# A scan kernel of two linear-attention mixers: the products of a chunk's last two levels are issued one visit later

## The chip, the cores and the metric

The kernel runs on one core of a Trainium2 chip. The core has a matrix engine (TensorE, PE in the profile; its weight loads are PEld), VectorE (DVE), ScalarE (ACT), GpSimd (POOL), and SyncE (SP), which issues the DMA transfers here. Each engine works through its own list of instructions in order and waits for the others by semaphores. The metric is the time on the device in microseconds (us), the median of several runs.

## What is computed

One layer of a backbone over 2048 latent tokens and 256 context tokens (D_MODEL 1024). After a modulated norm and one large projection, two mixers run in parallel, each in both directions over the tokens: gated linear attention (GLA, with a decay per key channel) and a gated delta rule (GDN). Their outputs are normalised, gated, merged and projected. Cut to the part that the change touches, the GLA recurrence of one direction and head is

```
S_t = diag(exp(g_t)) S_(t-1) + k_t v_t^T          # S: 64 x 128, g_t: log decay of each of the 64 key channels
o_t = q_t S_t
```

The kernel computes it by chunks of 128 tokens: o = (state before the chunk) + A v, where A[t,s] = sum over channels of q_t k_s exp(G_t - G_s), G being the running sum of g. The second direction is the same with the order of the tokens reversed.

## The kernel before

A Python program writes the work of each engine with generators that are woven together, and a scheduler then fixes the order of each engine's list. An order-only dependency can be added by `behind()`.

The time line has a projection (to about 1386 us of the span), the scan stage (`phase_mix`, 1386 to 1760) and the output stage (to the end). The scan stage has one *visit* for each of 16 steps, and in step s the forward scan takes a chunk from the front and the backward scan one from the back, so that in the first half (eight visits) outputs of chunks are written out to memory (`do<-oi`, `do<-og`, L1394) and in the second half, after the *turn*, they are read back (`oi<-do` L1388, `og<-do` L1382), added up and finished (`finish`: sums of squares fsq L1408 on ACT, logarithm and exponential of them L1409 and L1410, scaling on POOL L1411, transposes on PE L1415).

The matrix A of a chunk isn't formed by one product, since exp(G_t - G_s) can't be split into two safe factors over a whole chunk. It is made by *levels* m = 64, 32, 16, 8, 4, 2, 1: at level m, pairs of tokens that lie in neighbouring blocks of m are covered, with the decay taken relative to the border of the two blocks. For each pair of levels `gla_group` sums the gates on PE (L1124, with gates split into a high part gh, L132 on ACT, and a low part gl, L135 on POOL), takes exponentials on ACT (E, L1215), and multiplies them with q on DVE (ql, L1221) and with k on POOL (L1222). `gla_lev` multiplies the two on PE (L1263, four heads of 64 channels by halves of 64 tokens: 8 products a level) and puts each level's part into `own` by a masked copy on DVE (L1274); for m = 64 into `at` on ACT (L1271). Level 1 is done apart: `gla_ones` (transposes of g on PE L1233, exponential on ACT L1235, qk on DVE L1237 and POOL L1238) and `gla_near`, which sums qk with a matrix of ones columns on PE (L1245), puts it into `own` (L1247) and copies `own` to `at` (L1251). The gates' load is `g<-dg` (L1109).

In visit order `gla_step` does: the split of the gates, the chunk's ends (`gla_ends`, L1124, exponential L1133 on ACT), then for the chunk of the visit before `gla_near` and the gated state (`gla_state`, L1326 on PE), then the groups of levels 0-1 and 2-3, the output of the chunk before (`gla_out`, L1345 and L1353), the products of these four levels, then the group of levels 4-5 (m = 4 and 2), `gla_ones`, and the products of levels 4-5. Into this are woven the products of the other mixer (L1055, L1058 on DVE, L1066, L1077, L1087, L1096, L1084 on POOL).

Of the kernel before, what the change touches and what calls it, by code (L numbers as in the profile page):

```python
# [97 lines left out]
class Build:  # L98
# [1142 lines left out]
    def gla_near(self, r):  # L1241
        nc, at, own, w = self.nc, r["at"], r["own"], r["near"]
        pd = self.pe()
        for ct in range(2):
            nc.tensor.matmul(pd[:, 2 * ct:2 * ct + 2], w[:, ct], self.bones, start=True, stop=True)  # L1245
        B = [P, 4, 64]
        nc.vector.copy_predicated(own, self.am[:, len(LEVELS) - 2].unsqueeze(1).broadcast_to(B),  # L1247
                                  pd[:, 0:4].unsqueeze(2).broadcast_to(B))
        for x in range(2):
            half = slice(64 * x, 64 * x + 64)  # L1250
            nc.scalar.copy(at[half, :, half], own[half])  # L1251
# [25 lines left out]
    def gla_step(self, f, b, prev):  # L1277
        nc = self.nc
        self.gla_split(f)
        self.gla_split(b)  # L1280
        f["at"] = f["kp"].tile([P, 4, P], F32, name="at", bufs=1)
        own = f["own"] = f["kp"].tile([P, 4, 64], F32, name="own", bufs=1)
        nc.gpsimd.tensor_tensor(own, self.diag[:, f["c"] - NCTX, :].unsqueeze(2).broadcast_to([P, 4, 64]),
                                self.id64.unsqueeze(1).broadcast_to([P, 4, 64]), op=ALU.mult)
        yield
        self.gla_ends(f)
        yield
        if prev is not None:
            self.gla_near(prev[0])
            S = self.gla_state(prev)  # L1290
            yield
        levs = yield from self.gla_group(f, 0)
        self.gla_ends(b)
        yield
        more = yield from self.gla_group(f, 2)
        self.gla_kt(f)
        self.gla_qe(b)
        yield
        if prev is not None:
            out, done = self.gla_out(prev, S)  # L1300
        self.gla_lev(levs + more, out if prev is not None else None)
        if prev is not None:
            done()
            yield
            yield from self.gla_put(prev)
        yield
        last = yield from self.gla_group(f, 4)
        yield
        self.gla_kt(b)
        f["near"] = self.gla_ones(f)  # L1310
        self.gla_qe(f)
        yield
        self.gla_lev(last)
        yield
        if f["c"] == NCH - 1:
            self.gla_near(f)
        yield
# [580 lines left out]
```

## Time and profile before

| | |
|---|---|
| median of 3 runs | 2127.24 us (2123.59 to 2130.51) |
| the profiled execution | 2126.9 us, its span 2125.1 us, granted clock 0.987 |
| busy over the span | PE 2037.5 us (96%), PEld 1670.0 (79%), DVE 1282.5 (60%), ACT 914.1 (43%), POOL 818.2 (38%) |
| DMA | 346.97 MB, mean 163 GB/s; in the scan stage near 300 GB/s |

In the profile's rows the first number is the start in the span or, in rows of groups, the busy time; then the duration, the engine, the line, the operation with the tile written and the tiles read, the shape and the count; in brackets the engine's idle time just before and what ended it. In the chain of waits (the chain of work that ended last) a row is start, duration, and the engine or transfer with its line. A `DMA` row there is a transfer from its issue to its landing. In tables by window the columns stand in the head row; PEclk is the granted clock of PE as a share, DMA the busy share of the 16 DMA engines.

### The profile page before, as it was taken

What the parts mean: (1) busy time and instruction counts of PE and PEld (TensorE: products, weight loads), DVE (VectorE), ACT (ScalarE), POOL (GpSimd) and SP (SyncE); (2) the same over time, 40 slices, a digit from 0 to 9 for tenths busy, and PEclk for the clock granted to TensorE, in tenths of its full rate; (3) what the DMA queues carried; (4) which work ended last, traced back from release to release, by engine and by line L of the source; (5) the groups of instructions that cost most, each with busy time, mean ns of one, the idle gap of its engine ahead of it and who ended that gap; (6) DMA issues with size and microseconds to landing.
All of it is one profiled execution on the core that took longest, in us unless ns stands there. A gap on an engine that the chain in (4) does not pass through costs nothing.

```text
span 2125.1 us, 40362 instructions
## 1 busy us (share of the span) xinstructions
PE 2037.5 (96%) x15208; PEld 1670.0 (79%) x15208; DVE 1282.5 (60%) x2229; ACT 914.1 (43%) x2208; POOL 818.2 (38%) x746
## 2 busy tenths in 40 slices
PE   5999999999999999999999999899998898999998
PEld 2688888888888888777777777688887786787786
DVE  3814555566667663555555655467677786566776
ACT  3645254555553223444344444355555565002332
POOL 2410122222221104666566665266566655102211
PEclk9999999999999999999999999999999999999999
DMA  8323122222222224444444443688988887898543
GB/s 285 110 87 118 48 61 64 76 62 65 63 72 75 62 73 139 130 135 131 139 155 149 134 136 115 200 294 300 324 293 282 299 282 235 289 311 299 183 146 110
DMA packets 272863, 346.97 MB, mean 163 GB/s; under 512 B 25000, under 2 KB 176796, under 8 KB 272668
## 3 DMA queue, kind: packets, MB, share of 16 engines
q1 hardware_dynamic: 272668, 344.39, 49.2%
q8 instruction: 120, 1.97, 0.4%
q14 instruction: 75, 0.61, 0.1%
HBM read 218.73 MB, written 125.57 MB: 162 GB/s over the span
## 4 chain that ended last, share of the span: by engine, by line
PE 71%; DMA 9%; issue 6%; POOL 5%; DVE 4%; ACT 4%; SPq 1%; DVEq 0%; POOLq 0%; ACTq 0%
PE pz L371 46%; PE pm L1604 3%; DMA g<-dg 2%; PE pz L1604 2%; PE pe L943 1%; PE pl L1002 1%; PE pl L995 1%; PE pl L1003 1%; POOL E L1222 1%; DMA dm<-ga 1%; PE pe L1124 1%; PE pp L1822 1%; PE pq L620 1%; PE pz L1087 1%; PE pz L1077 1%
## 5 line engine op out<-in xcount | busy, mean ns | idle before, releaser
L371 PE MATMUL pz<-hi,wh 128*128 128x512 f32 (+1 forms) x1560 | 621.7, 399 | 1.1 <-DVE hi L134 1.1
L371 PE MATMUL pz<-lo,wh 128*128 128x512 f32 (+1 forms) x1560 | 600.6, 385 | 2.0 <-POOL lo L135 2.0
L371 PE MATMUL pz<-hi,wl 128*128 128x512 f32 (+1 forms) x1520 | 588.9, 387 | 0.0
L371 PEld LDWEIGHTS pz<-lo,wh 128*128 128x128 f32 x1560 | 294.8, 189 | 51.5 <-POOL lo L135 3.9
L371 PEld LDWEIGHTS pz<-hi,wh 128*128 128x128 f32 x1560 | 294.5, 189 | 47.3 <-DVE hi L134 1.7
L371 PEld LDWEIGHTS pz<-hi,wl 128*128 128x128 f32 x1520 | 286.1, 188 | 53.8 <-issue 0.4
L135 POOL TENSOR_TENSOR wl<-w,wh 128x1024 fp32r<-128x1024 f32 x44 | 109.6, 2493 | 436.5 <-ACT wh L132 312.0
L575 DVE SCALAR_TENSOR_TENSOR acc<-zpad,cw,acc 128x1024 f32<-128x1024 f32 x192 | 271.4, 1414 | 6.6
L880 DVE CAST_PREDICATED U<-kit,pl 128x256 f16<-128x256 int32 x216 | 91.2, 431 | 140.5 <-PE pl L1003 136.8
L996 ACT CAST ppb<-pl 128x256 f16<-128x256 f32 x216 | 73.6, 373 | 170.9 <-PE pl L995 158.6
L1604 PE MATMUL pm<-y,wb 128*128 128x512 f32 x480 | 117.7, 396 | 1.3 <-DVE ga L1607 1.2
L135 DVE TENSOR_TENSOR sql<-sq,sqh 128x512 fp32r<-128x512 f32 (+1 forms) x36 | 28.0, 805 | 141.3 <-ACT sqh L132 141.1
L1222 POOL TENSOR_TENSOR E<-E,ak 128x256 f32<-128x256 f32 x96 | 81.3, 866 | 78.1 <-ACT E L1215 40.6
L1604 PEld LDWEIGHTS pm<-y,wb 128*128 128x128 f32 x480 | 89.9, 189 | 23.0 <-DVE ga L1607 1.5
L630 POOL TENSOR_TENSOR acc<-acc,sq 128x512 f32<-128x512 f32 x32 | 51.3, 1611 | 137.8 <-ACT sq L629 89.9
L560 ACT COPY zpad<-pz 128x512 f32<-128x512 f32 x48 | 28.2, 587 | 137.5 <-PE pz L371 137.5
L1215 ACT ACTIVATE E<-pe 128x128 f32<-128x128 f32 x320 | 64.9, 308 | 42.6 <-PE pe L1124 42.1
L1124 PE MATMUL pe<-wt,gh 128*128 128x256 f32 x264 | 74.7, 313 | 4.5 <-ACT E L1133 2.7
L1002 PEld LDWEIGHTS <-Tm 128*128 128x128 f16 x864 | 55.5, 98 | 26.8 <-issue 22.2
L880 DVE CAST_PREDICATED Tm<-kit,pl 128x256 f16<-128x256 int32 x180 | 76.4, 424 | 0.0
L132 ACT CAST wh<-w 128x1024 fp32r<-128x1024 f32 x44 | 46.2, 1050 | 68.3 <-PE pz L371 56.0
L1221 DVE TENSOR_TENSOR ql<-E,q 128x256 f32<-128x256 f32 x96 | 66.9, 723 | 9.1 <-ACT E L1212 7.8
(326 smaller groups left out, 4259.3 us busy)
## 6 DMA issues: line engine op xcount, KB each, us to landing
gd<-dgd SPq DMA_DIRECT2D x32, 768.0 KB, 7.4
w<-in_w_in SPq DMA_DIRECT2D x44, 512.0 KB, 3.8
dgate<-ob SPq DMA_DIRECT2D x128, 128.0 KB, 1.8
qk<-dqkv SPq DMA_DIRECT2D x32, 512.0 KB, 6.1
ga<-dgate SPq DMA_DIRECT2D x64, 256.0 KB, 4.6
x<-in_x SPq DMA_DIRECT2D x28, 512.0 KB, 5.0
dqkv<-acc SPq DMA_DIRECT2D x192, 64.0 KB, 1.6
dgd<-tm SPq DMA_DIRECT2D x36, 256.0 KB, 2.5
```

What stands on the lines that cost most here:

```text
L135: getattr(nc, lo).tensor_tensor(dst_lo, src, dst_hi.bitcast(F32), op=ALU.subtract)
L371: nc.tensor.matmul(ps[:, 0:n], a[:, kk, :], b[:, kk, :], start=(k == 0), stop=(k == last - 1))
L575: nc.vector.scalar_tensor_tensor(acc, src, wcol, acc, op0=ALU.mult, op1=ALU.add)
L630: nc.gpsimd.tensor_tensor(v, v, r, op=ALU.mult)
L880: self.nc.vector.copy_predicated(out, mv, data)
L996: nc.scalar.copy(ppl, pc.rearrange("p h (j i) -> p h j i", i=m))
L1002: nc.tensor.matmul(pu[:, h], Tm[:, h], ppl[:, h], start=True, stop=True)
L1124: self.nc.tensor.matmul(out, g[:, i, ct * P:(ct + 1) * P], self.wt[:, d, cols[0]:cols[1]], start=(j == 0), stop=(j == 1))
L1215: nc.scalar.activation(E[:, ct, li, x].rearrange("p (j e i) -> p e j i", e=2, i=m), s[:, x * P:(x + 1) * P].rearrange("p (e j i) -> p e j ...
L1221: nc.vector.tensor_tensor(ql[:, li], E[:, :, li, 0], q, op=ALU.mult)
L1222: nc.gpsimd.tensor_tensor(E[:, :, li, 1], E[:, :, li, 1], k, op=ALU.mult)
L1604: nc.tensor.matmul(ps, self.wab[j // 2][wi][:, 4 * i + k, (j % 2) * P:(j % 2) * P + P], yy[:, k, :], start=(n == 0), stop=(n == 11))
```

## The change

The products of levels 4-5 (and the two masked DVE copies that follow them) are no longer issued at the end of the chunk's own visit, but in the next visit, inside `gla_near`, behind the two products with the ones columns and ahead of the gated state. The chunk's record keeps the group's result until then (`f["last"]`). For the last chunk, `gla_near` runs at the end of its own visit as before, and takes the products with it. The `behind` of the gated state on the last level product (`self.last_lev`) now means the moved products. In the changed file the lines between L1246 and L1313 have numbers higher by one (L1263 is L1264, L1274 is L1275, L1251 is L1252).

```diff
@@ gla_near
         for ct in range(2):
-            nc.tensor.matmul(pd[:, 2 * ct:2 * ct + 2], w[:, ct], self.bones, start=True, stop=True)
+            mm = nc.tensor.matmul(pd[:, 2 * ct:2 * ct + 2], w[:, ct], self.bones, start=True, stop=True)
+        self.gla_lev(r["last"], mm)
         B = [P, 4, 64]
@@ gla_step
         yield
-        last = yield from self.gla_group(f, 4)
+        f["last"] = yield from self.gla_group(f, 4)
         yield
         self.gla_kt(b)
         f["near"] = self.gla_ones(f)
         self.gla_qe(f)
         yield
-        self.gla_lev(last)
         yield
         if f["c"] == NCH - 1:
             self.gla_near(f)
```

How it moves instructions, in three places. First PE, from the end of one visit to the beginning of the next (lv is the products' PSUM tile, bones the ones columns). Before:

```order
L1055 MATMUL pz<-Sb_17905,qk 128x128
L1233 MATMUL pe<-kf,g_17738 128x128 x4
L1055 MATMUL pz<-Sb_17905,qk 128x128 x3
L1263 MATMUL lv<-ql,E 64x64 x16
L1055 MATMUL pz<-Sb_17919,qk 128x128 x4
L1124 MATMUL pe<-wt,gh_18113 128x256
L1124 MATMUL pe<-wt,gl_18114 128x256
L1124 MATMUL pe<-wt,gh_18113 128x256
L1124 MATMUL pe<-wt,gl_18114 128x256
L1245 MATMUL pe<-bones,qk_18048 128x2 x2
L1326 MATMUL pz<-av,akt 64x128 x8
```

and in the changed kernel:

```order
L1055 MATMUL pz<-Sb_17905,qk 128x128
L1233 MATMUL pe<-kf,g_17720 128x128 x4
L1055 MATMUL pz<-Sb_17905,qk 128x128 x3
L1055 MATMUL pz<-Sb_17919,qk 128x128 x4
L1124 MATMUL pe<-wt,gh_18095 128x256
L1124 MATMUL pe<-wt,gl_18096 128x256
L1124 MATMUL pe<-wt,gh_18095 128x256
L1124 MATMUL pe<-wt,gl_18096 128x256
L1245 MATMUL pe<-bones,qk_18048 128x2 x2
L1264 MATMUL lv<-ql,E 64x64 x16
L1326 MATMUL pz<-av,akt 64x128 x8
```

The block of 16 went past four L1055, the four L1124 of the next chunk's ends, and L1245. In most visits it is this one move; in the first two other products (L652) lie there in the place of L1055.

Second, the turn between the two halves of the scan, on ACT and on SP. ACT before, from one cast of gates to the copies at:

```order
L132 CAST gh_18913<-g_18887 128x256
L1135 COPY dec<-E_18215 128x2
L1215 ACTIVATE E<-pe 128x2x4x16 x2
L1215 ACTIVATE E<-pe 128x2x8x8 x2
L1215 ACTIVATE E<-pe 128x2x4x16 x2
L1215 ACTIVATE E<-pe 128x2x8x8 x2
L132 CAST gh_18497<-g_18469 128x512
L1144 COPY akt<-pe 128x256
L1271 COPY at<-lv 64x2x2x64 x2
```

and in the changed kernel (its tiles bear other numbers):

```order
L132 CAST gh_18895<-g_18869 128x256
L1135 COPY dec<-E_18215 128x2
L132 CAST gh_18479<-g_18451 128x512
L1215 ACTIVATE E<-pe 128x2x4x16 x2
L1215 ACTIVATE E<-pe 128x2x8x8 x2
L1215 ACTIVATE E<-pe 128x2x4x16 x2
L1215 ACTIVATE E<-pe 128x2x8x8 x2
L1144 COPY akt<-pe 128x256
L1272 COPY at<-lv 64x2x2x64 x2
```

The cast of the 128x512 gates went ahead of the eight exponentials. On POOL its counterpart gl (L135) went in the same way ahead of the two E products (L1222) that read these exponentials. SP before, at the same turn (do are the outputs in memory, with the chunk's number, first of oi, the other mixer's output, then of og):

```order
L1394 DMA do_7_14836<-og 128x512
L1394 DMA do_8_14837<-og 128x512
L1388 DMA oi<-do_8_14853 128x512
L1388 DMA oi<-do_7_14852 128x512
L1382 DMA og<-do_7_14836 128x512
L1382 DMA og<-do_8_14837 128x512
L1038 DMA gd<-dgd_8_151 128x1536
L1382 DMA og<-do_9_14838 128x512
L1382 DMA og<-do_6_14835 128x512
L1388 DMA oi<-do_9_14854 128x512
L1388 DMA oi<-do_6_14851 128x512
L1109 DMA g_18469<-dg_191 128x512
```

and in the changed kernel:

```order
L1388 DMA oi<-do_8_14853 128x512
L1394 DMA do_7_14836<-og 128x512
L1394 DMA do_8_14837<-og 128x512
L1388 DMA oi<-do_7_14852 128x512
L1038 DMA gd<-dgd_8_151 128x1536
L1382 DMA og<-do_8_14837 128x512
L1382 DMA og<-do_7_14836 128x512
L1382 DMA og<-do_9_14838 128x512
L1382 DMA og<-do_6_14835 128x512
L1388 DMA oi<-do_9_14854 128x512
L1388 DMA oi<-do_6_14851 128x512
L1109 DMA g_18451<-dg_191 128x512
```

The first reload, `oi<-do_8`, which has to wait for the landing of that chunk's write, went ahead of the two og writes.

Third, a visit of the second half on ACT, from the exponential of `gla_ones` to the first copies to at. Before:

```order
L1408 ACTIVATE fsq,fss<-oi 128x128 x2
L1133 ACTIVATE E_19352<-pe 128x512
L1408 ACTIVATE fsq,fss<-oi 128x128
L1135 COPY dec<-E_19352 128x2
L1409 ACTIVATE fss<-fss,cb 128x4
L1408 ACTIVATE fsq,fss<-og 128x128
L1410 ACTIVATE fss<-fss 128x4
L132 CAST gh_19733<-g_19705 128x512
L1408 ACTIVATE fsq,fss<-og 128x128
L1251 COPY at<-own 64x4x64
```

and in the changed kernel:

```order
L1135 COPY dec<-E_19334 128x2
L1408 ACTIVATE fsq,fss<-oi 128x128 x2
L132 CAST gh_19715<-g_19687 128x512
L1408 ACTIVATE fsq,fss<-oi 128x128
L1409 ACTIVATE fss<-fss,cb 128x4
L1408 ACTIVATE fsq,fss<-og 128x128
L1410 ACTIVATE fss<-fss 128x4
L1252 COPY at<-own 64x4x64
```

The cast went ahead of the last fsq of oi and the first of og; L1133 and L1135, the exponential of the next ends, went up as well. In the visits beside it the same cast moves by none to two fsq.

## The prediction

> **What bounds the kernel now.** I began with the busy time by engine in the window of the scan stage, then read PE's own timeline in one plain visit, then the waits by line, and last the chain of waits with the timelines of ACT, POOL and SP at the places where PE stands still. The stage runs from 1386 to about 1760 us of the span:
>
> ```profile
> core 0: us, PE busy (x) PEld busy (x) DVE busy (x) ACT busy (x) POOL busy (x), PEclk, DMA share, GB/s
> 1386.00:1760.00 374.00, 342.40 (x4548) 316.30 (x4546) 275.58 (x623) 213.89 (x908) 235.19 (x276) 0.98 0.85 294
> ```
>
> PE is busy 342.40 of 374.00 us, so all its standing still together is 31.6 us, and the DMA engines carry 0.85 of what they can. Here is PE, then POOL, in a plain visit of the first half:
>
> ```profile
> 1527.94 0.66 PE L1233 MATMUL pe<-kf,g 128*128 128x128 f32 x4
> 1528.43 0.83 PE L1055 MATMUL pz<-Sb,qk 128*128 128x128 f32 x6
> 1529.20 0.46 PE L1263 MATMUL lv<-ql,E 64*64 64x64 f32 x16
> 1530.01 0.46 PE L1263 MATMUL lv<-ql,E 64*64 64x64 f32 x16 [0.36 <-POOL E L1222]
> 1530.41 1.16 PE L1055 MATMUL pz<-Sb,qk 128*128 128x128 f32 x8
> 1531.32 0.36 PE L1124 MATMUL pe<-wt,gh 128*128 128x256 f32 x1
> ...
> 1531.88 0.51 PE L1245 MATMUL pe<-bones,qk 128*128 128x2 f32 x4
> 1532.31 1.09 PE L1326 MATMUL pz<-av,akt 128*64 128x128 f32 x16
> ...
> 1528.29 1.67 POOL L1222 TENSOR_TENSOR E<-E,ak 128x256 f32<-128x256 f32 x2 [2.56 <-ACT E L1215]
> 1530.39 0.73 POOL L1238 TENSOR_TENSOR qk<-qk,ak 128x256 f32<-128x256 f32 x1 [0.43 <-DVE qk L1237]
> ```
>
> The two L1263 rows are the block that moves (16 products in the code, 32 instructions here). From its start at 1529.20 to the next product at 1530.41 it holds PE for 1.21 us, of which 0.36 is a wait for POOL's second E, so 0.85 is work. The reader should also see that qk, which the ones products of L1245 need, leaves POOL at 1530.39 + 0.73 = 1531.12, while PE comes to L1245 only at 1531.88: 0.76 us of cover. The waits of these two lines over the whole stage:
>
> ```profile
> L1263 PE MATMUL lv<-ql,E 64*64 64x64 f32 x1536 | 35.3, 224 | 8.7 <-POOL E L1222 8.7
> L1245 PE MATMUL pe<-bones,qk 128*128 128x2 f32 x64 | 8.3, 233 | 1.0 <-POOL qk L1238 1.0
> ...
> 1625.13 0.46 PE L1263 MATMUL lv<-ql,E 64*64 64x64 f32 x16 [0.36 <-POOL E L1222]
> ```
>
> 8.7 us is all the waiting of L1263, first four levels included; the moved block has 0.36 in visits of either half of the stage, so about 15 visits x 0.36 = 5.4 us is what the change can take away there.
>
> **The change, part by part.** It adds and removes no instruction; 16 products and two DVE copies a visit go later, and the order of ACT, POOL and SP shifts round them.
>
> *The plain visits.* Without the block PE reaches L1245 at 1531.88 - 1.21 = 1530.67, but qk is ready at 1531.12, so there is a new wait of 0.45 in the place of the old one of 0.36. Then L1245 takes 0.43 (1531.88 to 1532.31) and the block its 0.85: L1326 starts at 1531.12 + 0.43 + 0.85 = 1532.40, where it was 1532.31. That is +0.09 a visit, eight visits +0.7. Against it L1124 comes 1.21 earlier, and the exponentials of the next chunk's ends with it. The bounds are -5.4 (every wait goes and none comes) and +0.7; I take 0, nearer to the row than to the hope. The two DVE copies now follow all eight rhs operations of L1058; the copies that wait for them feed L1345, late in the next visit, and I give them nothing.
>
> *The turn between the two halves, ACT and POOL.* The next rows are ACT, POOL and PE round the cast of one chunk's gates (gh), which waits for a load:
>
> ```profile
> 1583.30 1.47 ACT L1215 ACTIVATE E<-pe 128x128 f32<-128x128 f32 x8 [0.86 <-PE pe L1124]
> 1590.05 0.62 ACT L132 CAST gh<-g 128x512 fp32r<-128x512 f32 x1 [5.29 <-DMA g<-dg]
> ...
> 1584.96 1.77 POOL L1222 TENSOR_TENSOR E<-E,ak 128x256 f32<-128x256 f32 x2
> 1590.74 1.29 POOL L135 TENSOR_TENSOR gl<-g,gh 128x512 fp32r<-128x512 f32 x1 [4.00 <-ACT gh L132]
> ...
> 1590.19 1.11 PE L1263 MATMUL lv<-ql,E 64*64 64x64 f32 x64
> 1591.23 0.38 PE L1124 MATMUL pe<-wt,gh 128*128 128x256 f32 x1
> ...
> 1592.99 0.66 PE L1233 MATMUL pe<-kf,g 128*128 128x128 f32 x4
> ```
>
> Before, eight exponentials and the two E products on POOL are done by 1586.7, and ACT then waits 5.29 us with nothing behind it that anyone needs. Afterwards gh stands ahead of those eight exponentials and gl ahead of those two E. So with the same landing: gl ends at 1592.0, the two E take 1.77 to 1593.8, and the last 32 of PE's 64 products, about half of 1.11, end at 1594.3 where they ended at 1591.23. That is +3.1 for L1233. The lower bound is 0 (if PE is held by something else there; its next load was issued 0.8 us after L1233 ended, which may be slack); I take +2.5.
>
> *The same place, SP.* These are SP's issues, the chain's row for the write of og, the page's row for a write of the same size, and the window of the turn:
>
> ```profile
> 1571.44 1.27 SPq L1394 DMA_DIRECT2D do<-og  x2
> 1576.58 2.02 SPq L1388 DMA_DIRECT2D oi<-do  x2
> 1578.64 0.90 SPq L1382 DMA_DIRECT2D og<-do  x2
> 1583.36 0.38 SPq L1109 DMA_DIRECT2D g<-dg  x1
> 1594.38 2.86 SPq L1109 DMA_DIRECT2D g<-dg  x2
> ...
> 1572.18 6.96 DMA do<-og
> ...
> dgd<-tm SPq DMA_DIRECT2D x36, 256.0 KB, 2.5
> ...
> 1576.50:1580.00 3.50, 3.50 (x39) 3.33 (x38) 2.37 (x9) 1.44 (x4) 1.34 (x2) 1.00 0.68 179
> ```
>
> The first reload of oi was issued at 1576.58, when the write of that chunk had landed. Now it stands ahead of the two og writes, so these are issued about 1577.6 to 1578.2 and not 1571.44 to 1572.18, 6 us later, and the og reloads behind them, and the g of 1583.36 behind those, wait for their landing. With 6.96 for the landing g is 5.6 us later (a gd that now goes first gives 0.4 back); with the 2.5 of the quiet row it is 1.2. I take +2.5, nearer the quiet end, since the DMA share there is 0.68. A sentence on a page: the Trainium skill (Perfetto Trace Analysis, DMA Instruction — HWDGE (DVE, Sync)) says that the completion of a transfer that writes to HBM can be surprisingly late, because the semaphore's update comes behind the confirmed write. By that the landing would stay near the 6.96 of the chain's row, this term would be +5.6 and the sum 2137.5; the 2.5 of the page's row, also a write to HBM, speaks for less.
>
> What follows is bound by that g: the later load that is issued after L1233, its cast, and PE:
>
> ```profile
> 1601.88 0.62 ACT L132 CAST gh<-g 128x512 fp32r<-128x512 f32 x1 [5.03 <-DMA g<-dg]
> 1605.56 1.12 PE L1415 MATMUL pe<-kf,oi 128*128 128x128 f32 x4 [4.39 <-POOL oi L1411]
> 1605.50:1607.30 1.80, 1.74 (x8) 0.50 0.71 274
> ```
>
> ACT waits 5.03 and PE 4.39, so a late L1233 is not made up there; it goes through in full. The last row shows one thing more: after 4.39 us of standing PE's granted clock is 0.50. The new stall of 3 to 8 us at L1263 would bring the same, and PE's products from L1124 to the end of L1233, 1591.23 to 1593.65, are 2.4 us: at half the clock +2.4 at most, 0 if the clock stays; I take +1.0, between the two. The Trainium skill (TensorE: Matmul & The Clock Gate, What's actually happening) says that the clock falls to half after an idle window of about 3.4 us, which runs freely, and comes back after a busy one. The trace agrees in the 4.39; by the rule the whole 2.4 would come with any stall that is safely longer than a window, and the sum would be 2135.8.
>
> *The second half.* There the load of g, ACT's sums of squares (fsq) and POOL's scaling (L1411) set the pace, PE waits for them, and what PE gains in a visit is lost in that wait. ACT, and then the chain:
>
> ```profile
> 1655.40 0.30 ACT L1408 ACTIVATE fsq<-oi 128x128 bf16<-128x128 f32 x1
> ...
> 1656.03 0.29 ACT L1408 ACTIVATE fsq<-og 128x128 bf16<-128x128 f32 x1
> ...
> 1658.13 0.62 ACT L132 CAST gh<-g 128x512 fp32r<-128x512 f32 x1 [1.62 <-DMA g<-dg]
> ...
> 1663.07 1.05 POOL og L1411
> 1664.17 0.66 PE pe L1415 x4
> ...
> 1689.63 1.05 POOL og L1411
> ```
>
> Here the cast waits 1.62 for its load, with the fsq already done. Afterwards it stands one fsq of oi, one of og and two short functions earlier, and these, about 1.0 us (1655.40 to 1656.32, and the last short function), come behind the landing and ahead of the og that releases PE. In the next visit two fsq change sides (0.30 and a read-out each, an estimate of 0.8), in the one after one (0.4), and in the visit before two whose og I take to be covered for the most part (0.3). The sum is +2.5 at most, and 0 if the og products have cover in all of them; the og rows in the chain say that two of them don't, and I take +1.5.
>
> The sum: 0 + 2.5 + 2.5 + 1.0 + 1.5 = +7.5 us on the profiled execution of 2126.9 (span 2125.1, 1.8 around it), 2134.4. The median of the three runs is 2127.24, 0.3 above that execution, so I say 2134. A measurement of this kernel can tell about 0.3%, 6.4 us, from no change: faster is below 2120.9, slower above 2133.6.
>
> **The rivals.** *The new waits are covered and it comes out even.* For it: the block's wait only changes its name (0.36 for 0.45), and the g of the turn may land no later, when the og writes meet an emptier machine. Then the sum is 0 plus at most the second half's 2.5, 2127 to 2129. Against it: the 5.29 in front of the cast, behind which eight exponentials now stand.
>
> *It is faster: the next chunk's ends come 1.21 us sooner.* L1124 and the exponentials behind it move up by the whole block in each visit. If they, and not POOL's qk, set the pace in the first half, seven visits give 7 x 1.21 = 8.5 us, 2118; with only the old waits gone it is 2126.9 - 5.4 = 2121.5. It decides if qk is ready by 1530.7, in the place of 1531.12. Against it stands POOL's row, where qk itself waits 0.43 for DVE; and the loss at the turn would have to stay away.
>
> *It is much slower.* The two delays at the turn add up with their upper values, 3.1 + 5.6 + 2.4, and with the 2.5 and 0.7 they make +14.3, 2141. It decides if the og writes take their 6.96 again.
>
> **How the numbers follow.** The likeliest, delays at the turn and in the second half that go through, gets 0.50 with its own range of 2130 to 2139, of which 0.40 lies above 2133.6. Even: 0.28. Faster: 0.16, of it 0.14 below 2120.9. Much slower: 0.06. So faster 0.14, same 0.10 + 0.28 + 0.02 = 0.40, slower 0.46. The range that leaves out half of the fast end and the last of the slow one is 2121 to 2141.
>
> **What would show it.** In the profile afterwards: L1245 waits about 0.45 for POOL qk in the visits of the first half and the moved block not at all; the eight exponentials of the turn start after the gh that waits for its load, and PE stands 3 us or more within its 64 products there; SP issues the og writes after the first reload of oi, near 1577; the gh of 1601.88 starts about 5 us later; PE's waits for og at L1415 are longer by 0.5 to 1 in the visits after 1650. I am wrong if the g of the turn lands as before, or if L1245 waits for nothing and the visits of the first half are 0.4 us or more shorter each.

## The result, and the profile after

The changed kernel takes 2139.52 us (median of 8 runs, 2134.53 to 2144.58), the kernel before 2129.54 (8 runs, 2120.32 to 2131.70): the ratio is 1.0054, interval 1.0036 to 1.0072. It is slower by 10 us, where the prediction had 2134.0, within its range of 2121 to 2141 but too low. The profiled execution of the changed kernel is the slowest of its runs (span 2142.8, 2144.58 with what lies around it), so its visits hold some 15 us of loss and not 10.

The waits of PE in the scan stage, by line and cause (total us, times, longest), first of the kernel before and then of the changed one:

```profile
PE pe L1415 <- POOL oi L1411: 10.6, 3, 4.4
PE lv L1263 <- POOL E L1222: 8.7, 24, 0.8
PE pe L1415 <- POOL og L1411: 7.7, 6, 2.4
```

```profile
PE pe L1415 <- POOL oi L1411: 10.5, 4, 3.9
PE pe L1415 <- POOL og L1411: 10.2, 10, 3.4
PE pe L1245 <- POOL qk L1238: 7.5, 14, 1.0
PE lv L1264 <- POOL E L1222: 5.6, 12, 1.3
PE pz L1096 <- DVE Sb L1091: 4.1, 1, 4.1
PE pe L1233 <- ACT E L1215: 2.1, 1, 2.1
```

The reader sees two things. The moved products traded one wait for another: L1264's fell by 3.1 us, and L1245's came up from 1.0 to 7.5. (In the timeline no moved product waits any more; what is left at L1264 belongs to the first four levels.) And two large waits are new, one at L1096 and one at L1233, while the waits for og became more.

Where in the stage the time went is read from the start of L1345 (the first products of a visit's output) in PE's timeline. The table gives its start, less that of the kernel before, less the same difference in the first visit. Each row is one execution, and one execution says little: r4_all and s_sp have the same lists on ACT, DVE, POOL and SP up to the turn, and differ by 4.7 us at the eighth visit. So a step of a few us weighs only where several rows agree. The other kernels are explained with the experiments.

| kernel | visit 3 | 4 | 8 | 9 | 10 | 13 | 16 |
|---|---|---|---|---|---|---|---|
| changed | -0.8 | +3.4 | +6.2 | +12.2 | +9.0 | +12.3 | +14.8 |
| changed, cast of the fourth visit put back (r1_v4) | +0.8 | +3.0 | +4.8 | +9.5 | +6.6 | +6.2 | +7.9 |
| changed, cast of the turn put back (r2_turn) | -0.8 | +1.2 | +3.2 | +4.4 | +1.2 | +2.9 | +6.6 |
| changed, four casts of the second half put back (r3_half2) | -0.7 | +2.9 | +4.4 | +9.4 | +6.1 | +2.6 | +2.6 |
| changed, all six casts put back (r4_all) | +0.2 | +0.8 | +3.6 | +7.2 | +3.2 | +0.6 | +2.4 |
| the same, and SP's old order at the turn (s_sp) | +3.0 | +5.2 | +8.3 | +8.3 | +4.5 | +1.2 | +2.8 |
| before, all six casts moved up (x_pull) | -0.7 | +0.5 | +3.5 | +6.1 | +2.0 | +7.2 | +7.8 |
| before, first two casts moved up (x_pull1) | -0.4 | +1.1 | +3.6 | +7.6 | +3.9 | +4.4 | +4.8 |
| before, last four casts moved up (x_pull2) | -0.4 | -0.4 | +2.1 | +2.8 | +3.5 | +8.7 | +7.9 |

The changed kernel is 0.8 us ahead at the third visit, which one execution can't tell from nothing, and then loses in three places. (From the fourth visit to the eighth every row loses 1.5 to 3.1 us, those with nothing changed there too, so that part belongs to the one execution of the kernel before.)

**The fourth visit.** ACT and PE of the changed kernel, with two windows, and then ACT of the kernel before at the same place:

```profile
1464.12 0.62 ACT L132 CAST gh<-g 128x512 fp32r<-128x512 f32 x1 [1.60 <-DMA g<-dg]
1464.65 0.74 ACT L1272 COPY at<-lv 64x256 f32<-64x256 f32 x2
...
1466.26 0.65 PE L1233 MATMUL pe<-kf,g 128*128 128x128 f32 x4 [2.12 <-ACT E L1215]
...
1470.03 1.01 PE L1245 MATMUL pe<-bones,qk 128*128 128x2 f32 x4 [0.33 <-POOL qk L1238]
...
1472.04 1.97 PE L1326 MATMUL pz<-av,akt 128*64 128x128 f32 x16
...
core 0: us, PE busy (x) PEld busy (x) DVE busy (x) ACT busy (x) POOL busy (x), PEclk, DMA share, GB/s
1466.00:1470.00 4.00, 3.44 (x20) 3.15 (x20) 3.95 (x10) 1.96 (x11) 3.25 (x6) 0.69 0.97 309
1470.00:1476.00 6.00, 5.97 (x69) 5.51 (x70) 3.47 (x12) 1.30 (x5) 1.35 (x2) 0.64 1.01 385
```

```profile
1463.71 0.75 ACT L1271 COPY at<-lv 64x256 f32<-64x256 f32 x2
...
1466.36 0.71 ACT L132 CAST gh<-g 128x512 fp32r<-128x512 f32 x1
```

The cast of the gates has got ahead of the far copies in ACT's list (the two copies to at for level m = 64, L1272). Its load hasn't landed, so ACT stands 1.60 us, and the copies, the exponentials behind them and PE's L1233 stand with it (2.12 us). Then the granted clock falls: 0.69 from 1466 to 1470, so it fell ahead of the wait of 0.33 at L1245, and 0.64 in the next stretch, where L1326 takes 1.97 us and not 1.09. The visit is 4.2 us longer than before.

**The turn.** ACT, DVE, PE, a window of PE, and the cast of the next visit:

```profile
1595.04 0.62 ACT L132 CAST gh<-g 128x512 fp32r<-128x512 f32 x1 [6.82 <-DMA g<-dg]
1595.56 1.45 ACT L1215 ACTIVATE E<-pe 128x128 f32<-128x128 f32 x8
...
1596.53 0.74 DVE L1221 TENSOR_TENSOR ql<-E,q 128x256 f32<-128x256 f32 x1 [5.14 <-ACT E L1215]
1597.20 0.68 DVE L1091 TENSOR_TENSOR Sb<-Sb,pz 128x512 f32<-128x512 f32 x1
...
1597.93 2.08 PE L1096 MATMUL pz<-vn,gd 128*128 128x128 f32 x8 [4.14 <-DVE Sb L1091]
...
1597.90:1603.60 5.70, 5.67 (x49) 5.45 (x53) 2.19 (x4) 0.37 (x1) 2.90 (x3) 0.50 0.50 175
...
1611.86 0.62 ACT L132 CAST gh<-g 128x512 fp32r<-128x512 f32 x1 [0.91 <-DMA g<-dg]
```

The eight exponentials stand behind the cast, as forecast. But PE isn't stopped at its level products: DVE is, since its ql waits 5.14 us for those exponentials, and the other mixer's Sb (L1091) is queued behind ql on DVE; PE stops at L1096, which needs Sb, for 4.14 us. Then it runs at half clock for 5.7 us. The visit loses 6.0 us, and the next gives back 3.2, since its cast waits only 0.91 us for its load, where it waited 5.03. The net of the two visits is +2.8 here, +1.8 and +1.7 in the two other executions with this order on ACT (r1_v4, r3_half2), and -2.0, -0.4 and -3.8 in the three with the cast put back (r2_turn, r4_all, s_sp). In r4_all the visit itself still loses 3.6, so not all of the 6.0 is the cast's.

SP's issues there:

```profile
1581.41 0.32 SPq L1388 DMA_DIRECT2D oi<-do  x1
1581.82 0.86 SPq L1394 DMA_DIRECT2D do<-og  x2
...
1586.61 1.75 SPq L1382 DMA_DIRECT2D og<-do  x4
...
1589.56 0.38 SPq L1109 DMA_DIRECT2D g<-dg  x1
...
1606.63 0.98 SPq L1109 DMA_DIRECT2D g<-dg  x2
```

The og writes come 10 us later than in the kernel before (5.7 of which the stage was late already), but the og reloads follow 4.8 us behind their issue, where it took 7.2. The g of 1583.36 is issued 6.2 us later, 0.5 more than the stage's own delay. But it lands sooner: the cast that waits for it starts at 1595.04 and not 1590.05, 5.0 us later, 0.7 less than the stage's delay.

**The second half.** A visit near 1700 of the changed kernel, the cast and PE, and then the one of the kernel before:

```profile
1694.86 0.62 ACT L132 CAST gh<-g 128x512 fp32r<-128x512 f32 x1 [3.60 <-DMA g<-dg]
...
1698.11 0.66 PE L1415 MATMUL pe<-kf,oi 128*128 128x128 f32 x4 [3.49 <-POOL oi L1411]
...
1700.71 0.66 PE L1415 MATMUL pe<-kf,og 128*128 128x128 f32 x4 [0.83 <-POOL og L1411]
...
1702.48 0.66 PE L1415 MATMUL pe<-kf,og 128*128 128x128 f32 x4 [0.22 <-POOL og L1411]
```

```profile
1683.97 0.62 ACT L132 CAST gh<-g 128x512 fp32r<-128x512 f32 x1 [2.54 <-DMA g<-dg]
...
1686.98 0.66 PE L1415 MATMUL pe<-kf,oi 128*128 128x128 f32 x4 [3.05 <-POOL oi L1411]
...
1688.94 0.66 PE L1415 MATMUL pe<-kf,og 128*128 128x128 f32 x4 [0.19 <-POOL og L1411]
```

The cast waits 1.06 us more, about the work that now stands behind it, and PE's three waits make 4.54 us, where they made 3.24: 1.3 us for this visit, and 5.8 us from the tenth visit to the sixteenth. In the two other executions with these four casts moved and the products in their new place the table has 5.4 (r2_turn) and 1.3 (r1_v4).

### The profile page after: what moved, and what is told of

It is laid out like the page before. It is cut to its first block, busy times and chain, and to the rows that moved or that the text cites. A ratio compares the mean times of both kernels' runs of the same rounds, so it can differ in the third digit from the quotient of the medians.

```text
span 2142.8 us, 40340 instructions
## 1 busy us (share of the span) xinstructions
PE 2039.2 (95%) x15208; PEld 1673.7 (78%) x15208; DVE 1287.1 (60%) x2229; ACT 914.8 (43%) x2208; POOL 816.4 (38%) x746
## 3 DMA queue, kind: packets, MB, share of 16 engines
q8 instruction: 120, 1.97, 0.4%
## 4 chain that ended last, share of the span: by engine, by line
PE 69%; DMA 9%; issue 7%; POOL 6%; ACT 4%; DVE 3%; SPq 1%; DVEq 0%; POOLq 0%; ACTq 0%
PE pz L371 47%; DMA g<-dg 3%; PE pm L1604 2%; POOL E L1222 1%; PE pe L943 1%; DMA dm<-ga 1%; DMA ga<-dgate 1%; PE pl L1002 1%; PE pl L995 1%; PE pl L1003 1%; PE pe L1124 1%; PE pp L1822 1%; PE pq L620 1%; PE pz L1077 1%; PE pz L1604 1%
## 5 line engine op out<-in xcount | busy, mean ns | idle before, releaser
L135 POOL TENSOR_TENSOR wl<-w,wh 128x1024 fp32r<-128x1024 f32 x44 | 109.6, 2491 | 437.4 <-ACT wh L132 297.2
L135 DVE TENSOR_TENSOR sql<-sq,sqh 128x512 fp32r<-128x512 f32 (+1 forms) x36 | 28.0, 805 | 142.1 <-ACT sqh L132 141.9
L1222 POOL TENSOR_TENSOR E<-E,ak 128x256 f32<-128x256 f32 x96 | 82.4, 877 | 79.7 <-ACT E L1215 45.1
L1124 PE MATMUL pe<-wt,gh 128*128 128x256 f32 x264 | 74.2, 311 | 4.8 <-ACT E L1133 2.9
```

The costliest lines, as they stand in the source:

```text
L135: getattr(nc, lo).tensor_tensor(dst_lo, src, dst_hi.bitcast(F32), op=ALU.subtract)
L1124: self.nc.tensor.matmul(out, g[:, i, ct * P:(ct + 1) * P], self.wt[:, d, cols[0]:cols[1]], start=(j == 0), stop=(j == 1))
L1222: nc.gpsimd.tensor_tensor(E[:, :, li, 1], E[:, :, li, 1], k, op=ALU.mult)
```

## The experiments

All pins are order-only dependencies, which set the place of an instruction in its engine's list and add no wait. The theory Q: the casts' new places in ACT's list cost the time. The rival P: the moved products themselves cost it, by their new wait at L1245. A second rival S: SP's later writes. The line numbers of these kernels are higher by some lines. Each ratio is to the kernel before on the same chip. With a cast gh its counterpart gl (L135) or a scaling (L1411) changes place in POOL's list, so the runs test the two lists together and don't separate them.

**Casts put back, one place at a time and all together.** The edit (r4_all has all branches, the others some):

```diff
 def gla_step(self, f, b, prev):
-        self.gla_split(f)
+        hi = self.gla_split(f)                  # the cast gh, L132
+        if si == 4:
+            self.behind(hi, self.mark["e1"])    # r1_v4: last exponential of the visit's ones part
+        if si == 10:
+            self.behind(hi, self.mark["g2"])    # r2_turn: last of the eight exponentials
+        if si in (12, 13, 14, 15):              # r3_half2: 8th, 9th, 8th, 13th square sum
+            self.behind(hi, self.fsqp[{12: 8, 13: 9, 14: 8, 15: 13}[si] - 1])
```

> The changed kernel (2139.5 us) with one order-only dependency on ACT: in the visit whose L1233 waits 2.12 us, the cast gh of the next chunk goes back behind the exponentials of the ones part, where it stood before. Theory Q (the time is lost where a cast that waits for its load has got ahead of work in ACT's queue): PE's 2.12 us wait and the halved clock behind it go, 4.2 us less, about 2135.3. Theory P (the time is lost by the moved products themselves, their new wait of 0.55 us at L1245 in every visit): nothing changes, 2139.5.

Measured: 2137.04 us, ratio 1.0041 (1.0029 to 1.0052). That is not told apart from the changed kernel's 1.0054. In its profile the wait of L1233 is gone, but another is there, of the next chunk's L1124 (L1125 here), which the change has put ahead of the products that used to cover it:

```profile
1468.10 0.39 PE L1125 MATMUL pe<-wt,gl 128*128 128x256 f32 x1 [1.02 <-POOL gl L135]
```

So the expected 4.2 was too much: a wait of half the size of the removed stall (2.12) takes its place. And in this execution the clock fell to half behind it, as the rows that follow show. Below them are those of r4_all at the same place, with the same two waits, where the clock stayed:

```profile
1469.06 0.61 PE L1246 MATMUL pe<-bones,qk 128*128 128x2 f32 x4 [0.33 <-POOL qk L1239]
1470.62 1.97 PE L1329 MATMUL pz<-av,akt 128*64 128x128 f32 x16
...
core 0: us, PE busy (x), PEclk, DMA share, GB/s
...
1470.00:1475.00 5.00, 5.00 (x62) 0.69 0.97 372
```

```profile
1466.02 0.39 PE L1125 MATMUL pe<-wt,gl 128*128 128x256 f32 x1 [1.01 <-POOL gl L135]
...
1466.98 0.61 PE L1246 MATMUL pe<-bones,qk 128*128 128x2 f32 x4 [0.34 <-POOL qk L1239]
...
1468.15 1.09 PE L1339 MATMUL pz<-av,akt 128*64 128x128 f32 x16
...
1470.00:1475.00 5.00, 5.00 (x46) 1.00 0.97 385
```

The fourth visit lost 2.2 us in r1_v4 and 0.6 in r4_all.

> The changed kernel with one order-only dependency on ACT at the turn: the 128x512 cast stands again behind the eight exponentials, SP's order stays as changed. Theory Q: the 4.14 us for which PE waits at L1096 there and the halved clock behind it go; the visits slip by 0 instead of 2.8 us over the turn, and the load that comes 5 us later than before is covered, so about 2136.5 to 2137. Theory S (SP's later writes of og set the turn): nothing changes, 2139.5. Theory P: nothing changes.

Measured: 2134.69, ratio 1.0028 (1.0017 to 1.0040). The gain over the changed kernel is 4.8 us by the medians where 2.5 to 3 was expected, and the intervals just overlap; the wait at L1096 is gone.

> The changed kernel with order-only dependencies on ACT in four visits of the second half: the casts stand again behind the eighth, ninth, eighth and thirteenth square sum, as before the change. Theory Q: the 1.0 to 1.3 us that each of these visits is longer than before go, 3 to 5 us less, about 2135.5. Theory P: nothing changes, 2139.5.

Measured: 2131.37, ratio 1.0017 (1.0004 to 1.0030), clear of the changed kernel. By the medians it is the largest single part, 8 us (3 to 13 by the two intervals). In the table the second half no longer loses: it gains 3.5 us from the tenth visit to the sixteenth. PE in the visit shown above:

```profile
1685.83 0.66 PE L1425 MATMUL pe<-kf,oi 128*128 128x128 f32 x4 [2.04 <-POOL oi L1421]
1687.79 0.66 PE L1425 MATMUL pe<-kf,og 128*128 128x128 f32 x4 [0.19 <-POOL og L1421]
```

> The changed kernel with all six of these dependencies; the products stay where the change put them. Theory Q: all that the change costs goes, and the 1.3 us that the first three visits gained stay: 2128 to 2130, the time of before. Theory P: 2139.5. If the products' place costs a part, it lies between.

Measured: 2129.01, ratio 1.0003 (0.9992 to 1.0013). With the products where the change put them and the casts where they were, the time is that of before. P has fallen: the products' own move costs nothing that can be told, and gains nothing. In its waits one is traded for the other as in the changed kernel:

```profile
PE pe L1246 <- POOL qk L1239: 7.5, 14, 1.0
...
PE lv L1265 <- POOL E L1223: 4.9, 11, 1.0
```

Together these two lines have 12.4 us, where the kernel before has 9.7, and the time doesn't show the difference. The three parts alone gain 2.5, 4.8 and 8.2 us and together 10.5. With intervals of some 4 us to either side of each, that doesn't show whether they are additive.

**The reverse: the casts moved up in the kernel before.** Products untouched; the same places by dependencies the other way round (the far copies, the eight exponentials, the last square sums behind the cast).

> The kernel before, its products left where they were; only the casts gh of the next chunks are moved up in ACT's queue at the six places where the change had moved them (ahead of the far copies once, of the eight exponentials at the turn, of one or two square sums in four visits). Theory Q (the casts' places cost the time): 7 to 10 us slower than before, 2136 to 2139. Theory P (the products' place costs it): 2129.2, as before.

Measured: 2133.84, ratio 1.0027 (1.0016 to 1.0039): the casts alone make the kernel slower, by 6 us and not 7 to 10. Whether the rest of the changed kernel's 10 us needs the products' new place as well stays open, since the two intervals overlap.

> The kernel before, products in their old place, with only two casts moved up: the one ahead of the far copies in the fourth visit and the one ahead of the eight exponentials at the turn. In the run with all six moved up the profile slipped by 1.2 us in the fourth visit, and the 2.6 us lost at the turn were covered by the next load. Theory Q1 (each place costs only what the next wait doesn't cover): about 1 us more than before, no change that can be told. Theory Q2 (each place costs its stall in full): 4 us more.

Measured: 2131.51, ratio 1.0018 (1.0005 to 1.0032).

> The kernel before, products in their old place, with only the four casts of the second half moved up. Theory Q1 (the og behind one or two square sums releases PE, and nothing after it covers that): 4 to 6 us more than before, all that the run with six moved up showed. Theory Q2: 2 us more.

Measured: 2130.76, ratio 1.0023 (1.0009 to 1.0037). Either group alone costs about 4 to 5 us and both together 6. For the second half that is what Q1 said, and in the table it is 4.4 us from the tenth visit to the sixteenth. For the first two places the time is Q2's 4 us; the table has only 1.5 in the fourth visit and 0.3 net over the turn, which is Q1's, so the two don't agree.

**SP's order.** r4_all, with the reload of oi pinned behind the og writes:

> The kernel with all six casts put back (2129.0 us) and, besides, SP's order at the turn as before the change: both writes of og ahead of the first reload of oi. Theory S (the later writes of og cost time, as the prediction had it, 2.5 us): 2126.5. Theory Q (they land sooner on an emptier machine and the later wait covers the rest): 2129, no change.

Measured: 2127.07, ratio 0.9993 (0.9983 to 1.0003); it overlaps r4_all's, so a loss of 2.5 us by SP's order isn't shown, nor excluded (the difference is 0.0010, 2.1 us).

**Other places for the products, casts put back.** v_swap issues them ahead of the ones products; v_mid_pin ahead of L1124 as well, so that they pass only four L1055; v_mid_sp has SP's old order in addition. In v_swap the scheduler put SP's list at the turn back to the old order too (the og writes ahead of the first reload of oi), so it differs from r4_all in two things.

```diff
 def gla_near(self, r):
+        self.gla_lev(r["last"], ends)           # v_swap: behind the next chunk's L1124
         pd = self.pe()
         for ct in range(2):
             mm = nc.tensor.matmul(...)          # L1245
-        self.gla_lev(r["last"], mm)
...
 def gla_step(self, f, b, prev):
         yield
+        if prev is not None:                    # v_mid_pin, in the place of the line in gla_near
+            self.gla_lev(prev[0]["last"], self.mark["sb"])   # behind the second four L1055
         self.gla_ends(f)
```

> The casts put back as in the run with all six, and the moved products issued ahead of the two products with the ones columns and not behind them (still behind the next chunk's L1124). They are ready there, and POOL's qk has 0.85 us more to come: the new wait of 0.55 at L1245 goes. If PE sets the pace in the first half, eight visits x 0.45 = 3.6 us less than 2129.0, about 2125.4; if POOL or the loads set it, 2129.

Measured: 2122.82, ratio 0.9983 (0.9968 to 0.9999). Its waits:

```profile
PE lv L1266 <- POOL E L1223: 6.2, 12, 1.2
...
PE pe L1247 <- POOL qk L1239: 0.8, 1, 0.8
```

> The casts put back, and the products moved past nothing but four L1055 (PE: eight L1055, the products, L1124, the ones products, the gated state). The old wait of 0.36 goes since POOL's E is ready 0.15 us before PE comes, L1124 is not earlier than before and so not exposed to a late gl, and qk is ready 0.4 us before L1245. Eight PE-paced visits x 0.36 = 2.9 us less than before, about 2126.3; in the second half nothing. If the visits aren't PE-paced: 2129.

Measured: 2124.19, ratio 0.9981 (0.9970 to 0.9991). Its waits:

```profile
PE lv L1264 <- POOL E L1223: 5.8, 9, 2.2
...
PE pe L1246 <- POOL qk L1239: 1.1, 2, 0.8
```

Here the old wait has gone (8.7 to 5.8, what is left belongs to the first four levels) and no new one has come at L1245. Both are faster than before, by some 3.6 to 5 us where 2.9 to 3.6 was expected (v_swap's interval ends just below 1).

> The best order so far: products behind four L1055 and nothing else, the six casts put back, and SP's order at the turn as before the change. Without the last it took 0.9981 of the kernel before. If SP's order costs what the run that put it back showed (0.0010 less, not told from nothing), 0.997; if not, 0.998.

Measured: 2123.36, ratio 0.9984 (0.9971 to 0.9997). SP's order makes no difference that these runs could tell. The three are alike; v_mid_pin has the smallest interval.

## Why the prediction was right or wrong

Three steps failed. The forecast gave the fourth visit nothing, without a reason; it gave SP's order 2.5 us that no run shows; and it took 1.5 us for the second half, where the runs have 4 to 8. The path at the turn was another one as well. That 2134 still lies near the 2139.5 is luck in part, since the turn's 6.0 us came out as 2.8 while the two other places cost more than forecast.

**The plain visits: the trade of waits and its 0 were right, but a place was left out.** The forecast 0.45 at L1245 is 0.55 in the trace, the moved block waits for nothing, and r4_all, with this trade and SP's new order, is at 1.0003. What failed is the count of places: the working priced the cast's move at the turn and in the second half, and left out the fourth visit, where the same cast had gone ahead of the far copies in ACT's list. The list of three places ahead of the prediction lacks it too, though the move stood in the changed kernel's order. By the trace that visit lost 4.2 us, half of it the stall of 2.12 and the rest with the fallen clock. Its price isn't fixed: with the cast ahead the visit lost 4.2, 3.6 and 2.0 us (changed, r3_half2, r2_turn), with the cast put back 2.2, 0.6 and 2.2 (r1_v4, r4_all, s_sp). A part comes back as another wait, because L1124, moved ahead of its cover, then waits for gl; the sentence that gave L1124 1.21 us earlier as a gain missed that it also meets its own input earlier.

**The turn, ACT and POOL (+2.5): right in cause, wrong in the way.** The stall came, but over DVE's list: ql behind the exponentials, Sb behind ql, PE at L1096, an earlier place than the level products. It was 4.1 us. The half clock behind it, forecast at 1.0 and at most 2.4, cost some 2.8, an estimate from the window (5.67 us of work at 0.50). *SP (+2.5)* didn't come: the g was issued 0.5 us later than the stage but landed 0.7 sooner, which is the sign that the prediction had named for being wrong, and below the 1.2 that it had as the quiet end. What it had wrong is the wait for the og writes: their reload followed 4.8 us behind their issue and not 7.2. s_sp leaves some 2 us open. *"It goes through in full"* failed: 3.2 us of 6.0 came back in the next visit, because the wait of 5.03 us for the load, which the prediction took as a sign that nothing is made up, was itself the slack. Before, the second of its two g loads was issued 3 us after L1233 had ended (1594.38 + 2.86 is the end of the two); here it was issued within 0.4 us of that. Of 6.0 forecast for the turn 2.8 were left.

**The second half (+1.5): the mechanism was right and the term was mis-sized.** The prediction knew the amounts (0.3, 1.0, 0.8, 0.4 in the order of the visits, 2.5 in all) and cut them to 1.5 for cover. In the changed kernel's profile PE's waits at L1415 in these four visits are longer by 0.8, 0.7, 1.3 and 1.4, some 4.1 in all: the cover wasn't there in three of them, and one was over-priced. The table has 5.8 for this execution, 1.3 to 5.4 in others, 4.4 in x_pull2, and the time of r3_half2 is 8 us less; so it is about 4 to 8, and not known better.

**The rivals.** "The next chunk's ends come 1.21 us sooner" was not seen: r4_all has it and is at 1.0003. The other price of that rival, 5.4 us for the old waits alone, is nearly what v_swap and v_mid_pin gained (5.0 and 3.6) by another place for the block. The even rival fell with the result, but it is what r4_all shows for the products alone. On the clock, 0.50 followed the waits of 4.14 and 4.39. It also fell after 2.12 in the fourth visit and after 1.02 and 0.33 in r1_v4, and it stayed at 1.00 after the same 1.01 and 0.34 in r4_all, and after 1.85 and 1.30 in r2_turn. So the length of a wait doesn't decide alone. The Trainium skill (TensorE: Matmul & The Clock Gate, What's actually happening) asks for an idle window of about 3.4 us, which the 4.14 and 4.39 fill and the waits of 2.12 and 1.02 don't; here the measurement decides. By the same section of the Trainium skill the window runs freely, so that where a stall falls in it could matter; no run here shows the window itself.

## What to carry to other kernels

When a scheduler sets the lists, a moved block moves others: compare the whole list of each engine, and price every place where something that waits for a load has got ahead of work, not only those near the edit. Follow the stall through each engine's list in turn, since the victim may be another mixer's work that is queued behind it on DVE. And a block that covers a wait should be moved only past what doesn't need the cover: here the place four products later gained some 4 us, and the place ten products later gained nothing.

## What the runs showed of the hardware that was not expected

The two writes of og at the turn (256 KB each) were followed by their first reload 3.8 to 5.3 us after issue in the six executions with SP's new order, and 6.1 to 8.0 in the seven with the old one. In the kernel before the DMA engines moved 290 GB/s in that stretch, in the changed one 253, at busy shares of 0.86 and 0.90. The reload also stands behind others in SP's list, so these figures are upper bounds of the landing.

And the same two waits of PE, 1.0 and 0.3 us, were followed by a granted clock of 0.69 over the next 5 us in one execution and of 1.00 in another (r1_v4, r4_all). The visit cost 1.6 us more in the one, which is some 0.1% of this kernel's time.
